# A hybrid DeltaNet, band attention and MoE block: the order of the v and vb projections, of the modulation matvecs, of the z tiles, and the pieces of the last expert loads

## The chip, the cores and the metric

The kernel runs on one core of one Trainium2 chip. The time is the device time of one execution, in microseconds. The kernel before takes 1188.68 us, the median of three runs (1187.45 to 1189.12).

## What is computed

The reference is one transformer block on 256 tokens of width 1024, all in f32. A conditioning vector gives six modulation rows (shift, scale and gate for each of two halves). The first half mixes the tokens, the second is a mixture of experts:

```python
mod = silu(c) @ w_ada + b_ada                      # sh1, sc1, ga1, sh2, sc2, ga2
h = rms_norm(x, norm_w[0]) * (1 + sc1) + sh1
proj = h @ w_in                                    # A: q, k, v, z, alpha, beta;  B: q, k, v
o_a = gated_delta_rule(l2(q), l2(k), v, g, beta)   # silu(conv(q, k, v)); chunks of 64, 4 heads of 128
o_a = rms_norm(o_a, a_norm_w) * silu(z)
o_b = chunk_band_attention(q_b, k_b, v_b, rel_bias)  # 8 heads of 64
x = x + ga1 * rms_norm(concat(o_a, o_b) @ w_out, norm_w[1])
h = rms_norm(x, norm_w[2]) * (1 + sc2) + sh2
gates, experts = top4(h @ w_router + b_router)     # 32 experts
y = sum_e gate_e * (swiglu(h @ w_up[e] + b_up[e]) @ w_down[e] + b_down[e])
x = x + ga2 * rms_norm(y, norm_w[3])
```

## The kernel before, in words

**Buffers.** Ten fixed blocks of 2 MiB (w0, w1, wA to wH), each with an f32 and an f32r view of the same bytes, take every weight. In the first part they hold projection weights and scratch; later they are a ring for expert weights in the order wB, wA, w0, wE, wF, wD, wC, w1, wG, wH (`RINGTAGS`). PSUM has three pools of banks: "mm" (3), "dl" (3) and "tp" (2).

**The stream of projections** (`stream`, L413). Weights come in halves of 256 columns. `split` (L210) writes each half as a high part (ScalarE) and a low part (VectorE and GpSimd). One projection tile is `mm3` (L231): 24 matmuls of 256 columns. Sixteen tiles follow k and q: qb, kb, vb, v, four each, at positions 1 to 16; z has four more. v's tiles pass through a convolution into `vT`; vb's are only copied; vb's weights lie in wD, v's in w0, z's in w1. For every third half the high part lies in `whx`, the second half of wH (f32r); others lie in wG and the first half of wH, z's first half among these.

**The modulation chunks** (`lates`, L517). Eight 2 MiB chunks of `w_ada` are loaded and reduced by `modrow` (L484): 16 matmuls at L203, a copy, 4 small products at L208. Seven share wF, so a load waits for the matvec before it. `ADAPOS` names the tile position at which chunk i is loaded and its matvec is written, right behind each other.

**The delta rule** (`chain`, L533) is written after position 16, with high priority. After the decays it inverts a triangular matrix by six doublings in `pair_mm` (L638, matmuls L642, two "dl" banks each). After doublings 3 and 4, `ktv` (L649) transposes k (L653) and v (L657), the latter into a "dl" bank. Then come L706 and L709, the products L731 to L757, and the outputs `oa`.

**Attention** (`attention`, L760) first loads a strip of relative biases into the second half of wH (L762); GpSimd masks it (L764). Then nine steps: three `scores` (L776, two "mm" banks each; VectorE adds the strip at L781 and so frees the banks), three `trans` (L800), three `av` (L815). `mixed` (L859) lays z tiles between the steps: `ZPOS` [0, 2, 0, 0] puts three before the first step and one before the third. w_out's B half is loaded into wD (L857) and split into wF and wD; when z is done, its A half is loaded into w1 (L872) and split (`spa`, second part in the first half of wH). `wout_b` (L830) is four tiles of 12 matmuls. From L1051 on, `wout_a`, residual, router and the first gather stand in an order written out by hand for TensorE and VectorE.

**The experts.** 14 groups of two, one or four experts; a group has six steps j of weights (four up, two down), one 2 MiB block per expert and step. The first group's experts are fixed, so its loads need no routing, only free blocks. `LAST` cuts the loads of the last group into pieces, interleaved between its two experts.

Outside L1051 to L1094 each engine's order comes from a scheduler that plays the program through a timeline before the run: what was written earlier goes first among what is ready, and high priority goes before all. SyncE issues every DMA in one queue.

The change touches L30 to L35, L207 to L238, L387, L415 to L436, L513 to L518, L649 to L659 and L696.

Of the kernel before, what the change touches and what calls it, by code (L numbers as in the profile page):

```python
# [26 lines left out]
KV = 2  # L27
ADA = list("PPPPPPPP")
ADATAG = list("FFBFFFFF")
ADAPOS = [0, 2, -1, 4, 6, 8, 10, 12]  # L30
ADABANK = "tp"
KW = 2
ZPOS = [0, 2, 0, 0]

LAST = {3: (4, 4), 4: (4, 4), 5: (2, 2, 2, 1, 1)}  # L35


SINGLES, QUADS = 2, 3
# [11 lines left out]
def block_kernel(ctx, tc, x, small, rows, rel_ext, wpre, wexp, b_up, b_down, out,  # L50
# [35 lines left out]
    def wload(i, tag):  # L86
        t = block(tag)
        nc.sync.dma_start(t, wpre[i])
        return t.rearrange("p (k n) -> p k n", k=8)
# [108 lines left out]
    def colvec(w, vec, out_cols, tag="dl"):  # L198
# [8 lines left out]
        for m in range(4):  # L207
            T.matmul(out_cols[:, m:m + 1], ev[:, m * 128:(m + 1) * 128], ind, start=True, stop=True)  # L208

    def split(w, kv=None, steps=1, extra=None, copy=None):  # L210


        sr, wl = w
        kv = kv or KV
        wh = extra
        if wh is None:
            wh = highs[nsp[0] % 3]
            nsp[0] += 1
        kn = sr.shape[1]
        wh = wh.rearrange("p (k n) -> p k n", k=kn)  # L220
        st = kn // steps
        for k in range(0, kn, st):
            (copy or S.copy)(wh[:, k:k + st], sr[:, k:k + st])
            m = k + kv // steps
            V.tensor_sub(wl[:, k:m], sr[:, k:m], wh[:, k:m])
            w_ = max(1, 512 // sr.shape[2])
            for i in range(m, k + st, w_):
                G.tensor_sub(wl[:, i:i + w_], sr[:, i:i + w_], wh[:, i:i + w_])
        return wh, wl

    def mm3(b_, lhs, rhs, ks=8, late="l", first=True, last=True):  # L231


        low = (1, 0) if late == "l" else (0, 1)
        seq = [(i, j, k) for k in range(ks) for i, j in ((0, 0), (1 - low[0], 1 - low[1]))]
        seq += [(*low, k) for k in range(ks)]
        for n, (i, j, k) in enumerate(seq):
            T.matmul(b_, lhs(i, k), rhs(j, k), start=first and n == 0, stop=last and n == len(seq) - 1)  # L238

    blC = block("wC")  # L240
    qbT, kbT = [blC[:, 1024 * i:1024 * i + 1024].rearrange("p (h t) -> p h t", h=4) for i in range(2)]
# [105 lines left out]
    whx = h2(1)  # L347
# [36 lines left out]
        G.tensor_mul(zg[:, a, sl].rearrange("p (h d) -> p h d", h=2), zg[:, a, sl].rearrange("p (h d) -> p h d", h=2),  # L384
                     rw[:, None, R_AN:R_AN + 128].to_broadcast([P, 2, 128]))

    halves = [(nm, hf) for nm in ("k", "q", "qb", "kb", "vb", "v", "z") for hf in range(2)]  # L387

    def evac(nm, h, b_):
        if nm == "qb":  # L390
# [22 lines left out]
    def stream():  # L413

        def sp(n):  # L415
            if n < len(halves):
                nm, hf = halves[n]
                sps[n] = split(ws[nm][hf], extra=whx if n % 3 == 2 else None)

        def after(at):  # L420
            if at == ("qb", 3):
                ws["v"] = hload(9, "w0")
            if at == ("kb", 3):
                ws["z"] = hload(10, "w1")
            if at in (("q", 3), ("v", 3), ("z", 3)):
                flush()
# [5 lines left out]
        for part in range(2):  # L432
            if part:
                with tc.high_priority():
                    hpath(1)
                ws["vb"] = hload(8, "wD")  # L436
                sp(2)
            for h in range(4):
                wx, m = sps[h // 2], h % 2
# [70 lines left out]
            T.transpose(rb[:, m * 128:(m + 1) * 128], mcs[seg][:, 4 * hf + m:4 * hf + m + 1].to_broadcast([P, P]), ident)  # L510
        S.copy(dst[:, hf * 512:hf * 512 + 512], rb)

    def late(jobs):  # L513
        for i, tag in jobs:
            modrow(i // 2, i % 2, wload(11 + i, tag))

    def lates(pos):  # L517
        late([(i, "w" + ADATAG[i]) for i in range(8) if ADAPOS[i] == pos])  # L518

    bias_parts()  # L520
    st_ = stream()
# [11 lines left out]
    def chain():  # L533
# [113 lines left out]
        kdt, wT = mem.tile([P, 2, 512], F32, tag="ga2", name="kdt").rearrange("p i (h d) -> i p h d", h=4)  # L647

        def ktv(a):  # L649
            sl = slice(4 * a, 4 * a + 4)  # L650
            kp = bank("dl")
            for h in range(4):
                T.transpose(kp[:, h * 128:(h + 1) * 128], kqT[:, h, 0, a * 128:(a + 1) * 128], ident)  # L653
            V.tensor_mul((kdt, kw)[a], kp.rearrange("p (h d) -> p h d", h=4), (kd, ew)[a][:, :, None].to_broadcast([P, 4, 128]))
            vp = bank("dl")
            for h in range(4):
                T.transpose(vp[:, h * 128:(h + 1) * 128], vT[:, h, a * 128:(a + 1) * 128], ident)  # L657
# [12 lines left out]
        for s_ in range(1, 6):  # L670
# [23 lines left out]
                ktv(s_ - 3)  # L694
            yield 0.6
        qd = kqT[:, :, 1, 128:256]  # L696


        def both(dst, src, scale, r_):
# [710 lines left out]
```

## Time and profile before

| | us |
|---|---|
| median of three runs | 1188.68 |
| profiled execution, its own time | 1189.61 |
| its span, first to last instruction | 1187.8 |
| TensorE matmul busy | 1036.5 (87%) |
| VectorE, ScalarE, GpSimd busy | 315.4, 194.2, 94.4 |
| DMA: share of 16 engines | 90.8% |
| mean granted TensorE clock | 0.948 |

The terms of the prediction come from the profiled execution, which has 1.8 us around its span and lies 0.9 us above the median. Its first 260 us are projections, delta rule, attention and router; then come the experts, whose 192 blocks of 2 MiB are most of the 451.91 MB moved.

### The profile page before, as it was taken

The page shows a single profiled execution, that of the slowest core. Times are in us where ns is not written, and L with a number is a line of the kernel's source. Part 1 is how long each engine was busy: PE and PEld are TensorE (multiplying, and loading weights), DVE is VectorE, ACT ScalarE, POOL GpSimd, SP SyncE. Part 2 cuts the span into 40 slices and gives each one's busy share as a digit, 9 for nine tenths or more (in the row PEclk, how much of TensorE's full clock was granted, in tenths as well). Part 3 has the DMA queues.
Part 4 walks back from the last instruction along what each step waited for, and adds up shares of the span by engine and source line. Part 5 has one row for each costly group of instructions (what it writes and reads, how often), then busy time and mean ns, then how long its engine had stood idle before and what let it go on. Part 6 is the DMA issues. An engine that isn't in the chain of part 4 may idle for free.

```text
span 1187.8 us, 14569 instructions
## 1 busy us (share of the span) xinstructions
PE 1036.5 (87%) x5945; PEld 499.0 (42%) x5945; DVE 315.4 (27%) x802; ACT 194.2 (16%) x387; POOL 94.4 (8%) x89
## 2 busy tenths in 40 slices
PE   4899999899966799999977798999966799989986
PEld 2688888654321234434431142435421243324231
DVE  5476356454103022121211012122111011111112
ACT  3554335331000001010100001011000001010101
POOL 1546334100000000000000000000000000000000
PEclk9899999989987899999997899999987899999998
DMA  9936545769999999999999999999999999999993
GB/s 363 402 100 267 214 167 214 306 274 399 410 429 428 428 411 429 427 429 427 428 426 429 428 427 428 426 430 427 429 426 428 427 429 427 428 427 429 428 419 150
DMA packets 37348, 451.91 MB, mean 380 GB/s; under 512 B 4192, under 2 KB 5856, under 8 KB 8096
## 3 DMA queue, kind: packets, MB, share of 16 engines
q1 hardware_dynamic: 37280, 450.96, 90.8%
q8 instruction: 48, 0.79, 0.3%
q14 instruction: 20, 0.16, 0.0%
HBM read 449.50 MB, written 1.05 MB: 379 GB/s over the span
## 4 chain that ended last, share of the span: by engine, by line
PE 56%; DMA 38%; DVE 2%; ACT 2%; issue 1%; SPq 0%; POOL 0%; DVEq 0%; ACTq 0%
PE dl L1122 23%; DMA wA_f<-in_wexp_dram 11%; DMA wH_f<-in_wexp_dram 9%; PE mm L1122 9%; DMA wE_f<-in_wexp_dram 7%; PE mm L238 7%; DMA wD_f<-in_wexp_dram 6%; DMA w_f<-in_wexp_dram 3%; PE mm L1174 2%; PE tp L1011 2%; PE dl L642 2%; PE tp L203 1%; PE mm L442 1%; PE dl L238 1%; PE dl L203 1%
## 5 line engine op out<-in xcount | busy, mean ns | idle before, releaser
L1122 PE MATMUL dl<-w_f,xg 128*64 128x512 f32 (+2 forms) x224 | 108.6, 636 | 4.1 <-DMA w_f<-in_wexp_dram 4.1
L1181 DVE TENSOR_TENSOR acc<-acc,mm 128x512 f32<-128x512 f32 x50 | 34.4, 689 | 253.8 <-PE mm L1174 253.8
L1122 PE MATMUL mm<-w_f,xg 128*64 128x512 f32 (+1 forms) x208 | 92.4, 594 | 0.0
L1286 POOL TENSOR_TENSOR wC_f<-acc,m_row 128x512 f32<-128x512 f32 x2 | 2.5, 1276 | 934.0 <-DMA wA_f<-in_wexp_dram 934.0
L1140 ACT ACTIVATE sg<-gm 128x512 f32<-128x512 f32 x28 | 17.6, 630 | 298.6 <-DVE gm L1138 281.1
L1122 PE MATMUL dl<-wF_f,xg 128*64 128x512 f32 (+1 forms) x128 | 61.1, 622 | 4.0 <-DMA wF_f<-in_wexp_dram 4.0
L1122 PE MATMUL dl<-wD_f,xg 128*64 128x512 f32 (+1 forms) x128 | 60.4, 622 | 4.0 <-DMA wD_f<-in_wexp_dram 4.0
L1174 PE MATMUL mm<-yg,wts 128*128 128x512 f32 x108 | 52.6, 614 | 12.6 <-ACT yg L1172 12.6
L1122 PE MATMUL dl<-wA_f,xg 128*32 128x512 f32 (+1 forms) x96 | 51.2, 693 | 10.2 <-DMA wA_f<-in_wexp_dram 10.2
L1122 PE MATMUL dl<-wE_f,xg 128*64 128x512 f32 (+2 forms) x112 | 56.9, 662 | 3.6 <-DMA wE_f<-in_wexp_dram 3.6
L1122 PE MATMUL mm<-wB_f,xg 128*64 128x512 f32 (+2 forms) x128 | 57.2, 595 | 0.0
L1122 PE MATMUL mm<-wA_f,xg 128*64 128x512 f32 (+2 forms) x128 | 57.1, 595 | 0.0
L1122 PE MATMUL dl<-wB_f,xg 128*32 128x512 f32 (+1 forms) x96 | 52.7, 702 | 4.3 <-DMA wB_f<-in_wexp_dram 4.3
L1172 ACT COPY yg<-dl 128x512 f32<-128x512 f32 x28 | 16.4, 585 | 241.1 <-PE dl L1122 241.1
L1122 PE MATMUL dl<-wC_f,xg 128*64 128x512 f32 (+2 forms) x112 | 51.8, 610 | 3.9 <-DMA wC_f<-in_wexp_dram 3.9
L1011 PEld LDWEIGHTS tp<-oh,x 128*128 128x128 f32 x432 | 50.6, 194 | 7.6 <-issue 6.9
L1011 PE MATMUL tp<-oh,x 128*128 128x128 f32 x432 | 53.4, 280 | 0.0
L1122 PE MATMUL mm<-wE_f,xg 128*64 128x512 f32 (+1 forms) x112 | 49.8, 595 | 0.3 <-DMA wE_f<-in_wexp_dram 0.3
L1122 PEld LDWEIGHTS dl<-w_f,xg 128*64 128x64 f32 (+2 forms) x224 | 31.2, 144 | 40.5 <-issue 33.2
L1021 DVE TENSOR_SCALAR xg<-tp,mc,mc 128x128 f32<-128x128 f32 x52 | 19.6, 406 | 94.1 <-PE dl L1122 87.8
L1138 DVE TENSOR_SCALAR gm<-dl 128x512 f32<-128x512 f32 x14 | 9.7, 692 | 130.0 <-PE dl L1133 121.7
L1019 ACT ACTIVATE xg<-tp,mc,mc 128x128 f32<-128x128 f32 x52 | 21.8, 454 | 132.2 <-DVE xg L1021 132.2
(625 smaller groups left out, 2256.6 us busy)
## 6 DMA issues: line engine op xcount, KB each, us to landing
w_f<-in_wexp_dram SPq DMA_DIRECT2D x37, 2048.0 KB, 33.6
wF_f<-in_wexp_dram SPq DMA_DIRECT2D x19, 2048.0 KB, 31.6
wD_f<-in_wexp_dram SPq DMA_DIRECT2D x19, 2048.0 KB, 35.0
wE_f<-in_wexp_dram SPq DMA_DIRECT2D x19, 2048.0 KB, 36.0
wA_f<-in_wexp_dram SPq DMA_DIRECT2D x18, 2048.0 KB, 37.9
wB_f<-in_wexp_dram SPq DMA_DIRECT2D x18, 2048.0 KB, 33.6
wG_f<-in_wexp_dram SPq DMA_DIRECT2D x18, 2048.0 KB, 30.8
wC_f<-in_wexp_dram SPq DMA_DIRECT2D x18, 2048.0 KB, 32.3
```

The costliest lines, as they stand in the source:

```text
L203: T.matmul(b_[32 * i:32 * i + 32, :], vec[:, k:k + 1].to_broadcast([P, 32]), w[:, k, :], start=k < 4, stop=k >= 4)
L238: T.matmul(b_, lhs(i, k), rhs(j, k), start=first and n == 0, stop=last and n == len(seq) - 1)
L442: T.matmul(bs[h], wx[i][:, k, m * 128:(m + 1) * 128], hx[j][:, k, :], start=k + n == 0, stop=k == 7 and n == 2)
L642: T.matmul(b_[r_, c_ * 64:c_ * 64 + 64], lhs[r_, c_, :], id64[r_, :] if rhs is None else rhs[r_, c_, r_] if rhs is U else rhs[r_, c_, :], ...
L1011: T.matmul(b_[:, k * 128:(k + 1) * 128], x2[:, a, half(n)][:, k * 128:(k + 1) * 128], oh[:, a], start=a == tiles[0], stop=a == tiles[-1])
L1019: S.activation(xg[:, k], src, AF.Identity, scale=mc, bias=sc)
L1021: V.tensor_scalar(xg[:, k], src, mc, sc, op0=ALU.mult, op1=ALU.add)
L1122: T.matmul(b_[i * n:(i + 1) * n, :], lhs[:, k, i * n:(i + 1) * n], w(k), start=k == 0, stop=last and k == 7)
L1140: S.activation(sg, gm, AF.Sigmoid, scale=1.702)
L1172: S.copy(yg, b_)
L1174: T.matmul(cb, wt[:, a], yg, start=not (last and nn), stop=True)
L1181: V.tensor_add(acc[:, a, sl], acc[:, a, sl], cb)
```

## The change

Six edits. (1) v is projected before vb: v's weights go to wD, vb's to w0, so v has positions 9 to 12. (2) v's transposes and their products leave `ktv` and stand behind the last doubling, as `vtv`. (3) `ADAPOS` moves chunks 3 to 7 later, and each late chunk's matvec is written two positions behind its load (`ADALAG`). (4) That matvec is bound behind the last projection matmul written so far, `issue_after` (an order on TensorE alone, no wait). (5) `ZPOS` becomes [2, 4, 6, 8]: one z tile before the third, fifth, seventh and ninth step of attention. The condition on "z" in `sp` alters nothing, since z's halves are numbers 12 and 13 and only n % 3 == 2 is concerned. (6) In the last group the loads of j = 2 come in two pieces each instead of one, those of j = 4 in four instead of two.

```diff
-ADAPOS = [0, 2, -1, 4, 6, 8, 10, 12]
+ADAPOS = [0, 2, -1, 5, 7, 10, 12, 14]
+ADALAG = 2
-ZPOS = [0, 2, 0, 0]
+ZPOS = [2, 4, 6, 8]
-LAST = {3: (4, 4), 4: (4, 4), 5: (2, 2, 2, 1, 1)}
+LAST = {2: (4, 4), 3: (4, 4), 4: (2, 2, 2, 2), 5: (2, 2, 2, 1, 1)}
...
+    lastmm = [None]
...
-            T.matmul(b_, lhs(i, k), rhs(j, k), start=first and n == 0, stop=last and n == len(seq) - 1)
+            lastmm[0] = T.matmul(b_, lhs(i, k), rhs(j, k), start=first and n == 0, stop=last and n == len(seq) - 1)
...
-    halves = [(nm, hf) for nm in ("k", "q", "qb", "kb", "vb", "v", "z") for hf in range(2)]
+    halves = [(nm, hf) for nm in ("k", "q", "qb", "kb", "v", "vb", "z") for hf in range(2)]
...
-                sps[n] = split(ws[nm][hf], extra=whx if n % 3 == 2 else None)
+                sps[n] = split(ws[nm][hf], extra=whx if n % 3 == 2 and nm != "z" else None)
...
-                ws["v"] = hload(9, "w0")
+                ws["vb"] = hload(8, "w0")
...
-                ws["vb"] = hload(8, "wD")
+                ws["v"] = hload(9, "wD")
...
-    def late(jobs):
-        for i, tag in jobs:
-            modrow(i // 2, i % 2, wload(11 + i, tag))
+    lw = {}
 
     def lates(pos):
-        late([(i, "w" + ADATAG[i]) for i in range(8) if ADAPOS[i] == pos])
+        for i in range(8):
+            if ADAPOS[i] == pos:
+                lw[i] = wload(11 + i, "w" + ADATAG[i])
+            if ADAPOS[i] + (ADALAG if ADAPOS[i] >= 0 else 0) == pos:
+                if lastmm[0] is None:
+                    modrow(i // 2, i % 2, lw[i])
+                else:
+                    with tc.issue_after(lastmm[0].ins if hasattr(lastmm[0], "ins") else lastmm[0]):
+                        modrow(i // 2, i % 2, lw[i])
...
         def ktv(a):
-            sl = slice(4 * a, 4 * a + 4)
...
+        def vtv(a):
+            sl = slice(4 * a, 4 * a + 4)
             vp = bank("dl")
...
         qd = kqT[:, :, 1, 128:256]
+        for a in range(2):
+            vtv(a)
```

## Rows read from the trace of the kernel before

**Rows 1.** Stretches: PE, PEld, DVE, ACT, POOL busy (x instructions), PE clock, DMA share, GB/s.

```profile
57.00:221.00 164.00, 163.58 (x1637) 140.17 (x1638) 95.63 (x211) 74.06 (x151) 70.86 (x58) 1.00 0.51 192
...
260.00:265.00 5.00, 5.00 (x20) 1.58 (x18) 0.00 (x0) 0.34 (x1) 0.00 (x0) 1.00 0.00 0
...
600.00:800.00 200.00, 167.98 (x832) 63.28 (x825) 34.30 (x78) 16.12 (x32) 0.00 (x0) 0.93 1.01 428
```

**Rows 2.** SyncE's queue, timeline: the first load into a block that an expert freed.

```profile
265.66 0.33 SPq L1113 DMA_DIRECT2D wB_f<-in_wexp_dram  x1
```

**Rows 3.** TensorE, timeline: k's transposes of the third doubling, and the fourth doubling.

```profile
132.53 0.66 PE L653 MATMUL dl<-ident,kqT 128*128 128x128 f32 x4
...
158.14 1.15 PE L642 MATMUL dl<-wE_f,lmrow 64*64 64x64 f32 x32
```

**Rows 4.** The bias strip: SyncE's wait (ns, then start in us); GpSimd's mask, timeline.

```profile
L762 SPq EVENT_SEMAPHORE  x1: 22945/22945/22945, 151.4 to 151.4; - x1
...
180.51 1.49 POOL L764 TENSOR_SCALAR wH_f<-wH_f 64x512 f32<-64x512 f32 x1 [1.31 <-DMA wH_f<-in_rel_ext_dram]
```

**Rows 5.** TensorE, timeline: last reads of whx (first row), of z's part in wH (second).

```profile
161.63 0.72 PE L238 MATMUL mm<-wA_r,wH_r 128*128 128x256 f32 x4
...
173.07 1.20 PE L238 MATMUL mm<-wH_r,wA_r 128*128 128x256 f32 x8
```

**Rows 6.** A matvec and scores on TensorE (timeline); GpSimd's share of wD's splits (group).

```profile
163.47 1.92 PE L203 MATMUL tp<-wF_f,csil 128*32 128x512 f32 x16
...
182.70 1.57 PE L776 MATMUL mm<-wC_f 64*128 64x128 f32 x12
...
L228 POOL TENSOR_TENSOR wD_r<-wD_f,wF_r 128x512 fp32r<-128x512 f32 x4 | 5.2, 1301 | 19.4 <-DVE wD_r L225 16.0 <-PE mm L238 3.3
```

**Rows 7.** TensorE in the first tiles of wout_a (timeline), and one stretch with its clock.

```profile
227.82 3.69 PE L238 MATMUL dl<-wH_r,wC_r 128*128 128x512 f32 x8 [2.63 <-POOL wH_f L919]
...
232.26 1.98 PE L238 MATMUL mm<-wG_r,wC_r 128*128 128x512 f32 x8
...
228.00:230.00 2.00, 2.00 (x5) 1.63 (x6) 0.00 (x0) 0.00 (x0) 0.00 (x0) 0.50 0.99 426
```

**Rows 8.** Timeline: load of w_out's A half, a run of wout_b, the last split.

```profile
192.12 1.09 SPq L94 DMA_DIRECT2D w_f<-in_wpre_dram  x2
...
202.70 2.14 PE L238 MATMUL mm<-wF_r,wC_r 128*128 128x512 f32 x8
...
209.21 1.27 POOL L228 TENSOR_TENSOR w_r<-w_f,wH_r 128x512 fp32r<-128x512 f32 x1
```

**Rows 9.** TensorE in the last group, timeline, to its last expert matmul.

```profile
1137.21 0.38 PE L1133 MATMUL mm<-bup,sel 96*64 96x512 bf16 x1
...
1140.08 0.64 PE L1122 MATMUL dl<-wD_f,xg 128*64 128x512 f32 x1 [0.26 <-DMA wD_f<-in_wexp_dram]
...
1154.09 0.38 PE L1133 MATMUL dl<-bup,sel 96*64 96x512 bf16 x1
1155.98 0.66 PE L1150 MATMUL tp<-ident,gm 128*128 128x128 f32 x4 [1.50 <-DVE gm L1144]
...
1174.05 0.59 PE L1122 MATMUL dl<-wA_f,aT__5966 128*64 128x512 f32 x1
```

**Rows 10.** When j = 3 is whole (TensorE's weight load waits for its last piece).

```profile
1150.23 0.14 PEld L1122 LDWEIGHTS dl<-w_f,xg 128*64 128x64 f32 x1 [0.29 <-DMA w_f<-in_wexp_dram]
```

**Rows 11.** A load of 512 KiB and its time to landing; the last load, likewise; GB/s.

```profile
L1113 SPq DMA_DIRECT2D wA_f<-in_wexp_dram x1: 333/333/333, 1155.0 to 1155.0; - x1
...
DMA to landing us min/median/max: 12.4/12.4/12.4
...
L1113 SPq DMA_DIRECT2D wA_f<-in_wexp_dram x1: 337/337/337, 1162.6 to 1162.6; - x1
...
DMA to landing us min/median/max: 7.4/7.4/7.4
...
1160.00:1165.00 5.00, 5.00 (x20) 1.50 (x19) 0.00 (x0) 0.00 (x0) 0.00 (x0) 1.00 0.95 365
```

## The prediction

> **What bounds the kernel now.** I read the table of stretches first. From 600 to 800 us the DMA engines are full at 428 GB/s; TensorE is not. From 57 to 221 us it is the other way round: TensorE is busy 163.58 of 164 us, DMA half of the time [rows 1]. Next the two are tied together. The ten blocks of the ring fill before any expert runs; from 260 to 265 us nothing moves [rows 1], and SyncE issues the next load at 265.66, when the first expert's matmuls have freed a block [rows 2]. From there the stream is nearly unbroken to the end, so the date of that first free block sets the end, and TensorE sets that date. A microsecond that TensorE loses or gains before 265 us is one of the whole; loads that come a few microseconds earlier or later are not. Last I read the timeline of the final group: TensorE ends its expert matmuls at 1174.6 us [rows 9], while the last load, issued at 1162.6, lands 7.4 us later, at 1170.0 [rows 11]. There TensorE lags the DMA by 4.6 us, and 3.7 of these can be won at most, since the last piece still needs four matmuls, 0.9 us at the pace of j = 2 and 3, two times 32 matmuls from 1140.08 to 1154.5 [rows 9].
>
> So two places count: TensorE's queue before 221 us, and the last 40 us.
>
> **The change, part by part.**
>
> v before vb, v's transposes behind the doublings. Today the doublings stop: k's transposes of the third stand at 132.5 us, the fourth begins at 158.1, when v exists [rows 3]. The change removes that stop. It is worth nothing by itself: TensorE did other tiles meanwhile, it is full, and no instruction goes away. The loads of v and vb swap blocks with equal bytes and equal positions. What it does is move the delta rule's work ahead of tile 16, and so tile 16 and all that hangs on it some 10 us later. Sum: 0; if the cover went, the two transposes and products would cost a few tenths.
>
> The matvecs, two positions later and bound. The count is the same, 1.92 us for each run of 16 matmuls [rows 6]. 2 MiB take 4.9 us at 428 GB/s [rows 1]; two tiles are 48 matmuls, at 8 in 1.2 us [rows 5] some 6 to 7 us, with chain work between. Bounds: nothing (no wait of TensorE on wF stands in the trace now) and 2 us in all, if landings come late; I take 0. A load in SyncE's queue still waits for the matvec before it, and behind it stand the w_out load and the strip, which are not ready earlier. But the last chunk's matvec now follows tile 16, and wF is the block that takes w_out's high part; so the splits of w_out's B half, with four GpSimd pieces of 1.3 us [rows 6], move from the stretch before the strip into the stretch in which the strip arrives.
>
> The z tiles, later. This is where I expect the loss. The strip's load waited 22.9 us, to 174.4 [rows 4]. Its own half of wH, whx, was last read at 162.4; what ended at 174.3 were z's matmuls on the other half [rows 5]. The same pattern stands at 227.8: TensorE waits 2.63 us for GpSimd's write of the second half of wH before it reads the first [rows 7]. So the two views of wH are ordered as one object. Today three z tiles come first and run while the strip loads. After the change the strip comes first, two z tiles must wait for it and its mask, and the scores, ahead of z in priority, take all three "mm" banks, which only VectorE's addition of the strip gives back. From the strip's issue at 174.35 to the end of its mask are 7.6 us [rows 4]; about 1.0 of it lies before tile 16 ends (the last 8 matmuls no longer read whx), so 6.6 us remain. In them TensorE has the matvec, 1.9, and 20 of the 32 score matmuls, 2.6 at 12 in 1.57 us [rows 6]: a gap of 2.1 us. Bounds: 0, if the rest of the delta rule is still there to fill it, and 7.3, if all four GpSimd pieces (5.2 us) run ahead of the mask. I take 2.1, since some of the delta rule will fill it and some pieces will stretch it. After the 2.63 us of idling at 227.8 the clock stood at 0.50, its 1.2 GHz level, and eight matmuls took 3.69 us for 1.98 [rows 7]: 1.7 us more. After a gap of this size I take 0.6, between 0 and 1.7. Sum: +2.7.
>
> The rest of attention has z and wout_b for cover, some 23 us of TensorE work, against engines that work through three jobs of scores; I take 0. Loads for the experts that become late here have about 9 us, the idle stretch to 265.66, to hide in.
>
> The last group. j = 2 in halves lets TensorE start at 1137.6 rather than 1140.08 [rows 9], but j = 3 is whole only at 1150.2 [rows 10], and half of it has then still to run; today it ends at 1154.5 [rows 9]. So j = 2 brings 0.4. j = 4 in quarters brings more: TensorE waits 1.50 us at 1155.98 for the second half of the activation [rows 9], and with quarters the first two of eight steps of j = 4, 1.7 us of matmuls, have landed by then and fit there. Together 1.9; bounds 0.4 (the queue's order keeps the wait) and 3.7 (above). The six more issues cost SyncE 0.33 us each [rows 2]; it runs 7 us and more ahead, so they are hidden.
>
> Small pieces could slow the stream. From 1150.2 to 1167.4 [rows 10, 11] seven MiB land, j = 4 and six pieces of 512 KiB: 427 GB/s, the full rate; only with the 256 KiB pieces does a stretch show 365 [rows 11]. The Trainium skill (DMA: Bandwidth & Descriptors, Rules for kernel authors) asks for at least 1 MiB per DMA for full bandwidth, which speaks against this edit. By that rule the sum would lose the 1.9 and by the row it keeps them; the trace does not bear the rule out.
>
> **Sum.** +2.7 - 1.9 = +0.8 us. The profiled execution (1189.61) lies 0.9 above the median, so 1190.4 there and 1188.7 + 0.8 = 1189.5 in the median.
>
> **The rivals.**
>
> (a) The gap is covered: the delta rule's last products, or a queue order that keeps z where it was (the change then does not do what it says), fill it. For it: the whole delta rule has high priority, and TensorE idled only 0.4 us in 164 [rows 1]. Then only the last group counts: 1186.8, and 1185.0 with its best bound.
>
> (b) The gap is wide and the kernel slower. One mechanism: GpSimd takes w_out's pieces ahead of the mask. Two pieces make the gap 4.7, with the half clock 1.7 after it: +4.5 net, 1193.2; all four 1195.8. It decides when the gap and what the clock costs pass 4.3 us. For it: the splits are written before attention and so go first. Against it: they wait for the matvec and for ScalarE.
>
> (c) w1 is late. From the load of w_out's A half, at the end of z, to its last split are 18.4 us today [rows 8]. With z at the end of attention the cover is the last av and wout_b, 48 matmuls at 8 in 2.0 us [rows 8], about 13 us. Up to 5 us of wait plus the clock, less the last group: about 1192.8. Against it: z's matmuls fill any idle moment and will not all stand last.
>
> (d) The small pieces run at 365 GB/s [rows 11]: j = 4 takes 11.5 us for 9.9, and the last group brings 0.3 for 1.9: 1191.1. The rule above says this; the landings say otherwise.
>
> **How the numbers follow.** Forecast 0.42, (a) 0.28, (b) 0.20, (c) 0.08, (d) 0.02. A measurement of this kernel can tell about 0.2%, 2.4 us, from no change. The forecast's own range is 1187.0 to 1192.0: 0.05 of it is faster, 0.28 the same, 0.09 slower. (a) gives 0.17 to faster and 0.11 to the same, where the last group brings less than 2.4. (b) and (c) give 0.26 to slower and 0.02 to the same, (d) 0.02 to the same. Faster 0.22, the same 0.43, slower 0.35. The range takes in (a) to near its best bound and (b) with two to three pieces: 1185.6 to 1194.5.
>
> **What would show it.** In the profile after: the fourth doubling right behind the third, and the delta rule's last matmuls before tile 16 ends or soon after (step one). No z matmul between the strip's issue and its mask, and TensorE idle there by about 2 us, the mask named as releaser or VectorE's addition behind it, with a lower clock after it. The first free block's load at about 268.4 instead of 265.66. In the last group no wait at the second transposes and the last expert matmul about 2 us nearer to the last landing. If TensorE has no gap before 221 us, (a) holds; if the load of the first free block is at 270 or later, (b) or (c), told apart by whether the time went at the strip or before wout_a. The prediction is wrong altogether if that load comes earlier than 265, since I see nothing that lets TensorE finish the first part sooner.

## The result, and the profile after

The changed kernel takes **1200.35 us** (median of 4 runs, 1200.09 to 1204.13) against 1188.42 us for the kernel before on the same chip (4 runs). The ratio is 1.0109, 95% interval 1.0093 to 1.0126: slower by about 1%, 11.9 us by the medians and 13.0 by the ratio. The forecast was 1189.5 us, in a range of 1185.6 to 1194.5.

The profiled execution took 1200.43 us, its span is 1198.3 us, 10.5 longer than before. The first question is where that lies. The date that set the end before, the first load into a block that an expert freed [rows 2], has moved from 265.66 to 277.50 us (SyncE's timeline of the changed kernel):

```profile
277.50 0.33 SPq L1126 DMA_DIRECT2D wB_f<-in_wexp_dram  x1
```

That is 11.84 us, more than the whole loss. The last expert matmul, at 1174.05 before [rows 9], comes 10.4 us later (TensorE, last group, changed kernel):

```profile
1161.73 0.64 PE L1135 MATMUL dl<-w_f,xg 128*64 128x512 f32 x1 [0.51 <-DMA w_f<-in_wexp_dram]
...
1184.02 1.02 PE L1135 MATMUL dl<-wA_f,aT__5966 128*64 128x512 f32 x2
```

It ends at 1185.04, before it ended at 1174.64. So the last group, or what lies between, gave back 1.4, and the 1.50 us wait for the second half of the activation [rows 9] is gone. The loss is all ahead of 277.50. One row per kernel over the stretch from 57 us to that load says what kind of time it is (columns as in [rows 1]); first the kernel before, then the changed one:

```profile
57.00:265.66 208.66, 201.27 (x1843) 166.53 (x1843) 118.15 (x301) 87.73 (x189) 73.42 (x60) 0.97 0.57 221
```

```profile
57.00:277.50 220.50, 208.23 (x1832) 167.91 (x1829) 115.54 (x299) 86.00 (x189) 71.92 (x59) 0.96 0.54 210
```

TensorE runs the same program in both (1843 and 1832 records; a few are missing from a trace), but is busy for 7.0 us more and idle for 12.27 us in place of 7.39, which is 4.9 more. Nothing was added to its work, so the longer busy time has to be the same matmuls spread over more time. Two groups of instructions give most of it. The late matvecs, over this stretch (instructions | busy us, mean ns | idle before), before and after:

```profile
L203 PE MATMUL tp<-wF_f,csil 128*32 128x512 f32 x112 | 14.5, 599 | 0.0
```

```profile
L204 PE MATMUL tp<-wF_f,csil 128*32 128x512 f32 x112 | 19.7, 600 | 0.0
```

The mean of one matmul is the same, 600 ns, the group is 5.2 us longer: fewer of them ran side by side. The timeline of the changed kernel shows why:

```profile
154.60 1.04 PE L204 MATMUL tp<-wF_f,csil 128*32 128x512 f32 x2
155.57 1.14 PE L651 MATMUL dl<-wB_f 64*64 64x64 f32 x16
156.65 0.55 PE L668 MATMUL dl<-ident,wB_f 128*128 128x128 f32 x3
157.12 1.05 PE L204 MATMUL tp<-wF_f,csil 128*32 128x512 f32 x4
158.11 0.55 PE L668 MATMUL dl<-ident,wB_f 128*128 128x128 f32 x3
158.58 1.90 PE L204 MATMUL tp<-wF_f,csil 128*32 128x512 f32 x10
```

A whole matvec is 16 records in 1.92 us [rows 6]. Here one is cut into 2, 4 and 10, because the delta rule's matmuls, of high priority, stand between; two records alone take 1.04 us. The second group are the doublings (L642 before, L651 after): 15.2 and 7.4 us before, 16.1 and 7.7 after in their two large forms, 1.2 us more, in the same manner: 32 records together take 1.15 us at [rows 3], and 16 alone 1.14 (155.57, above). That leaves 0.6 us of the 7.0. The lower mean clock (0.96 for 0.97) accounts for about as much: its low level costs 2.4 us at the strip (below), where it cost 1.7 at 227.82 [rows 7].

The idle time stands in two places. The first is the strip (timeline of all engines):

```profile
183.59 1.05 PE L769 MATMUL dl<-lmrow,wE_f 128*128 128x128 f32 x8
...
185.91 1.12 PE L241 MATMUL mm<-w_r,wA_r 128*128 128x256 f32 x8
186.15 0.39 SPq L775 DMA_DIRECT2D wH_f<-in_rel_ext_dram  x1
...
192.96 1.49 POOL L777 TENSOR_SCALAR wH_f<-wH_f 64x512 f32<-64x512 f32 x1 [32.48 <-DMA wH_f<-in_rel_ext_dram]
194.47 1.89 DVE L794 TENSOR_TENSOR w_f<-mm,wH_f 128x512 f32<-128x512 f32 x3 [11.38 <-POOL wH_f L777]
195.22 1.81 PE L789 MATMUL mm<-wC_f 64*128 64x256 f32 x4 [3.21 <-DVE w_f L794]
...
196.96 3.78 PE L241 MATMUL mm<-wH_r,wA_r 128*128 128x256 f32 x16
200.54 1.91 PE L241 MATMUL mm<-w_r,wA_r 128*128 128x256 f32 x8
...
204.29 2.18 PE L241 MATMUL mm<-wH_r,wA_r 128*128 128x256 f32 x16 [0.18 <-DVE w_f L794]
```

The delta rule's last products (L769) run at 183.6, before tile 16 has ended (L241, 185.91). In the kernel before they are L756 and follow the attention's last matmuls (L815), and the copy behind them ended at 213.06:

```profile
210.25 1.09 PE L815 MATMUL mm<-w_f,wC_f 128*64 128x128 f32 x14
211.27 1.16 PE L756 MATMUL dl<-lmrow,wE_f 128*128 128x128 f32 x8
```

The strip's load is issued at 186.15, when tile 16 has read its block for the last time; before it was 174.35. From there the strip has to land, be masked and be added, and TensorE stops for 3.21 us. In the next five microseconds it has nearly its low level of clock, 1.2 GHz; the z tile at 196.96 and its last eight matmuls at 200.54 take 3.78 and 1.91 us there, the same work later 2.18 (204.29) and 1.12 (210.56), 2.4 us less:

```profile
190.00:195.00 5.00, 2.02 (x14) 1.54 (x14) 0.53 (x1) 2.38 (x2) 1.49 (x1) 1.00 0.17 57
195.00:200.00 5.00, 4.78 (x18) 4.00 (x19) 5.00 (x10) 1.75 (x9) 2.27 (x2) 0.55 0.01 2
```

The second place is ahead of the fourth tile of `wout_b`. w_out's A half is loaded when z's last tile has read w1, at 218.79 for 192.12 [rows 8]; its last split, GpSimd's, ends at 237.56, and ScalarE's copy of a finished tile of `wout_b` (L851) waits for it, since that split reads the first half of wH and the copy writes the second:

```profile
234.96 2.60 POOL L231 TENSOR_TENSOR w_r<-w_f,wH_r 128x512 fp32r<-128x512 f32 x2 [4.62 <-DVE w_r L228]
...
237.60 1.08 ACT L851 COPY wH_f<-mm 128x512 f32<-128x512 f32 x2 [1.96 <-POOL w_r L231]
...
238.24 2.12 PE L241 MATMUL mm<-wF_r,wC_r 128*128 128x512 f32 x8 [3.23 <-ACT wH_f L851]
```

This takes the place of the stop of 2.63 us at 227.82 [rows 7].

### The profile page after: what moved, and what is told of

It is laid out like the page before. It is cut to its first block, busy times and chain, and to the rows that moved or that the text cites. A ratio compares the mean times of both kernels' runs of the same rounds, so it can differ in the third digit from the quotient of the medians.

```text
span 1198.3 us, 14596 instructions
## 1 busy us (share of the span) xinstructions
PE 1042.6 (87%) x5945; PEld 492.0 (41%) x5945; DVE 313.6 (26%) x802; ACT 194.1 (16%) x387; POOL 94.6 (8%) x89
## 3 DMA queue, kind: packets, MB, share of 16 engines
HBM read 449.50 MB, written 1.05 MB: 376 GB/s over the span
## 4 chain that ended last, share of the span: by engine, by line
PE 65%; DMA 27%; DVE 4%; ACT 2%; issue 1%; POOL 0%; SPq 0%; ACTq 0%; DVEq 0%; POOLq 0%
PE dl L1135 27%; PE mm L1135 12%; DMA wH_f<-in_wexp_dram 9%; DMA wA_f<-in_wexp_dram 8%; PE mm L241 7%; DMA wE_f<-in_wexp_dram 4%; PE mm L1187 3%; PE tp L1024 3%; DMA wD_f<-in_wexp_dram 3%; PE dl L651 2%; DMA w_f<-in_wexp_dram 2%; PE tp L204 2%; PE tp L1163 1%; PE dl L204 1%; ACT yg L1185 1%
## 5 line engine op out<-in xcount | busy, mean ns | idle before, releaser
L1135 PE MATMUL dl<-wA_f,xg 128*32 128x512 f32 (+1 forms) x96 | 46.9, 644 | 10.5 <-DMA wA_f<-in_wexp_dram 10.5
L1135 PE MATMUL dl<-wB_f,xg 128*32 128x512 f32 (+1 forms) x96 | 48.5, 654 | 3.8 <-DMA wB_f<-in_wexp_dram 3.8
L1135 PE MATMUL mm<-wH_f,xg 128*64 128x512 f32 (+1 forms) x96 | 42.4, 594 | 0.3 <-DMA wH_f<-in_wexp_dram 0.3
```

The lines of the kernel that those rows point to most:

```text
L1135: T.matmul(b_[i * n:(i + 1) * n, :], lhs[:, k, i * n:(i + 1) * n], w(k), start=k == 0, stop=last and k == 7)
```

## The experiments

The theories on trial. **A**: the loss is made of several pieces. It splits in two: **A1**, the pieces themselves (cut matvecs, doublings in smaller runs), and **A2**, TensorE's order: since v no longer holds the delta rule back, its end goes ahead of the last projection tiles; these, the strip and the attention come later, and the delta rule's end, which had stood beside the attention, is used up (A2 took this form after the first round). **B**: w_out's A half, loaded late. **C**: the binding makes TensorE wait for a matvec's load. **D**: v's order costs by itself, whatever else is done.

All ratios are against runs of the kernel before on the same chip. The microseconds are the ratio minus one, times 1188.4; the last four columns are dates in the profiled execution, one for each kernel; that of e2 took 4.1 us more than its kernel's median, e12's 2.7 and e5's 2.5 more, e16's 2.4 less.

| kernel | ratio (95%) | us | strip issued | delta rule ends | attention's last matmul ends | first freed block |
|---|---|---|---|---|---|---|
| before | 1 | 0 | 174.4 | 213.1 | 211.3 | 265.7 |
| the change | 1.0109 (1.0093 to 1.0126) | +13.0 | 186.2 | 185.3 | 221.9 | 277.5 |
| e1 change, z tiles back | 1.0176 (1.0159 to 1.0193) | +20.9 | 195.3 | 185.7 | 230.2 | 284.1 |
| e2 change, matvecs whole | 1.0067 (1.0050 to 1.0084) | +8.0 | 184.3 | 184.4 | 217.8 | 275.9 |
| e3 change, matvecs back | 1.0091 (1.0074 to 1.0107) | +10.8 | 189.1 | 191.9 | 219.9 | 277.2 |
| e4 v's order alone | 1.0121 (1.0104 to 1.0138) | +14.4 | 195.0 | 191.2 | 228.8 | 278.7 |
| e5 v's order, strip freed | 1.0056 (1.0040 to 1.0073) | +6.7 | 147.2 | 189.5 | 222.6 | 271.6 |
| e6 change, strip freed | 1.0001 (0.9990 to 1.0013) | +0.1 | 145.5 | 187.3 | 215.6 | 265.5 |
| e7 before, strip freed | 0.9960 (0.9947 to 0.9972) | -4.8 | 139.7 | 212.1 | 210.3 | 259.1 |
| e8 last group alone | 0.9992 (0.9982 to 1.0001) | -1.0 | 174.6 | 213.5 | 211.7 | 266.0 |
| e9 change, v's order back | 1.0025 (1.0010 to 1.0040) | +3.0 | 160.1 | 206.3 | 209.0 | 267.5 |
| e10 z tiles alone | 1.0051 (1.0034 to 1.0068) | +6.1 | 161.7 | 212.9 | 213.0 | 269.6 |
| e11 matvecs alone | 0.9982 (0.9971 to 0.9992) | -2.1 | 171.9 | 205.6 | 209.1 | 259.7 |
| e12 change, whole and freed | 0.9938 (0.9916 to 0.9960) | -7.4 | 142.7 | 184.6 | 213.8 | 261.1 |
| e13 hold, misplaced | 1.0114 (1.0099 to 1.0130) | +13.5 | 189.0 | 188.1 | 224.1 | 279.9 |
| e14 before, freed, matvecs, last group | 0.9940 (0.9926 to 0.9953) | -7.1 | 139.4 | 208.4 | 211.7 | 259.3 |
| e15 as e14, matvecs whole | 0.9922 (0.9908 to 0.9935) | -9.3 | 137.1 | 207.6 | 211.6 | 257.4 |
| e16 change, v held | 1.0044 (1.0031 to 1.0058) | +5.2 | 170.5 | 196.9 | 211.3 | 268.2 |

**First round: which part is it?**

**e1**, z tiles back:

```diff
-ZPOS = [2, 4, 6, 8]
+ZPOS = [0, 2, 0, 0]
```

> The changed kernel with the four z tiles back at their old places (two ahead of the attention's third step, as before); all else as changed. Theory A (the loss is made of several pieces: late matvecs cut apart by the delta rule's matmuls, about +4.9 us; TensorE's idle 3.2 us and the half clock behind it, about +3.3 us, where the z tiles no longer stand in front of the strip; the doublings' own matmuls in smaller pieces, about +1.2): the stop at 190 to 195 us and the half clock at 195 to 205 us go, the matvecs stay cut, so 1193.5 to 1195.5 us. Theory B (all of the loss is w_out's second half, loaded only when the last z tile has read its block): the whole loss goes, about 1188.5 us, with the gain between 220 and 245 us. Theory C (the binding makes TensorE wait for the matvecs' loads): no change, about 1200 us.

Measured: 1208.14 us, eight more, the wrong side of all three theories. SyncE's wait for the strip (ns, then start) grows from 6953 to

```profile
L775 SPq EVENT_SEMAPHORE  x1: 15640/15640/15640, 179.6 to 179.6; - x1
```

because z's tiles, now ahead of the strip again, read the other half of wH, as before [rows 5]. They do not cover the strip; they delay it. With v first, the later z tiles are a gain.

**e2**, matvecs whole (`colvec`, only the late ones):

```diff
+            with tc.high_priority() if tag == "tp" else contextlib.nullcontext():
-            T.matmul(b_[32 * i:32 * i + 32, :], vec[:, k:k + 1].to_broadcast([P, 32]), w[:, k, :],
-                     start=k < 4, stop=k >= 4)
+                T.matmul(b_[32 * i:32 * i + 32, :], vec[:, k:k + 1].to_broadcast([P, 32]), w[:, k, :],
+                         start=k < 4, stop=k >= 4)
```

> The changed kernel with the eight matmuls of a late matvec given the same high priority as the delta rule's, so that nothing is put between them (all eight matvecs stand whole in TensorE's queue; their loads and the binding as changed). Theory A: about 0.95 us less for each of the six cuts, so 1195 to 1196.5 us, with a matvec's 16 records at 1.9 us each and the rest of the loss (the strip's stop) still there. Theory B (w_out's late load): no change, 1199.5 to 1201 us. Theory C (binding makes TensorE wait): no change or slower, 1200 us or more.

Measured: 1196.64 us, 5.0 less than the change by the ratios, as A had it. The group of matvecs, at 19.7 us in the change, now has

```profile
L206 PE MATMUL tp<-wF_f,csil 128*32 128x512 f32 x112 | 13.5, 598 | 0.0
```

So a cut matvec costs what the timeline says, but that is a part only; 8 us of loss remain.

**e3**, matvecs back:

```diff
-ADAPOS = [0, 2, -1, 5, 7, 10, 12, 14]
-ADALAG = 2
+ADAPOS = [0, 2, -1, 4, 6, 8, 10, 12]
+ADALAG = 0
...
-                if lastmm[0] is None:
+                if True:
```

> The changed kernel with the matvecs where they were (old places, no lag behind the load, no binding); v's order, the z tiles and the last group as changed. Two cuts are left in place of six. Theory A: 4 cuts fewer, 1196 to 1197.5 us, with the strip's stop still there. Theory C (lag and binding are what costs): about 1189 us. Theory B: no change, 1199.5 to 1201 us.

Measured: 1198.77 us, 2.1 less than the change by the ratios, with intervals that overlap. Theory C is out: without lag and binding nearly all of the loss stays. A's range, 1196 to 1197.5, is missed too: the matvecs take 15.5 us for 19.7, as it had them, but the doublings 16.9 and 8.5 us, 1.6 more.

**e4**, v's order alone: `halves`, the two `hload`s and `vtv` as in the change, put into the kernel before.

> The kernel before with v's tiles ahead of vb's and v's transposes behind the doublings, and nothing else of the change: matvecs, z tiles and the last group as before. Theory A: two more cuts of matvecs (+1.9) and smaller pieces of the doublings (+1.2) against an earlier start of the projections (-1.75): 1188.5 to 1191 us. Theory B and C: as before, 1188.4 us. If v's order itself is what costs (rival D: the delta rule without its stop takes TensorE from the projections, whatever the matvecs do): 1195 us or more.

Measured: 1202.70 us. This run carries the round: v's order by itself costs 14.4 us, more than the whole change, as theory D had it (1195 or more) and far above A's 1188.5 to 1191. The pieces are less than a third of it: its matvecs take 15.5 us, 1.0 more than before, its doublings 17.6 and 8.5, 3.5 more. What stands out is the stretch beside the attention, the same 30 us in the kernel before and in e4:

```profile
200.00:230.00 30.00, 26.95 (x169) 22.59 (x168) 13.59 (x44) 13.91 (x38) 7.32 (x6) 0.96 0.77 306
```

```profile
200.00:230.00 30.00, 21.21 (x125) 16.41 (x124) 20.64 (x55) 18.08 (x60) 13.79 (x13) 0.77 0.38 145
```

TensorE is idle for 8.8 us instead of 3.1, at a clock of 0.77, while VectorE and ScalarE work through the attention.

**Second round: the strip.** The strip is made free of what holds it. The halves of wH become objects of their own, and the last projection tile's high part goes to another buffer than the strip's half, so that the strip is loaded 35 us earlier in the kernel before (e7) and 41 to 48 earlier in the others (e6, e5):

```diff
+    hH = [[nc.alloc_sbuf_tensor_at(f"wH{i}_{d_}", (P, 2048), dt, offset=base + 16384 * 9 + 8192 * i).ap()
+           for d_, dt in (("f", F32), ("r", F32R))] for i in range(2)]
-    highs = [fixed["wG"][1][:, 0:2048], fixed["wG"][1][:, 2048:4096], fixed["wH"][1][:, 0:2048]]
+    highs = [fixed["wG"][1][:, 0:2048], fixed["wG"][1][:, 2048:4096], hH[0][1]]
...
-        return fixed["wH"][dt][:, 2048:4096]
+        return hH[1][dt]
...
-                sps[n] = split(ws[nm][hf], extra=whx if n % 3 == 2 else None)
+                sps[n] = split(ws[nm][hf], extra=whx if n % 3 == 2 and n < 11 else None)
```

**e5**, on v's order alone:

> v's order alone, as in the run that cost 14.5 us, but with the attention's strip freed: the two halves of block wH are objects of their own, so that the strip no longer waits for reads of the other half, and the last projection tile's high part no longer lies in the strip's half, so that the strip can be loaded from about 150 us on. Theory A2 (v's order lets the delta rule run ahead of the last projection tiles; the strip's load, which waits for those tiles, is issued at 195 in place of 174 us and nothing is left to stand in front of it): the stops and half clocks between 200 and 230 us go, about 8.8 - 3.0 us of idle PE and some 5 us of half clock, so 1189 to 1192 us. Theory A1 (cut matvecs and doublings in small pieces are the loss): 1199 us or more.

Measured: 1194.92 us, half of the loss. The strip is there at 152, but TensorE still stops, now for the attention's own steps:

```profile
205.00:210.00 5.00, 2.65 (x24) 1.88 (x24) 4.64 (x21) 5.00 (x19) 1.77 (x3) 1.00 1.04 441
210.00:215.00 5.00, 2.04 (x8) 1.43 (x8) 4.71 (x14) 3.67 (x6) 2.12 (x3) 0.66 0.61 262
215.00:220.00 5.00, 4.45 (x22) 3.62 (x23) 3.71 (x6) 1.90 (x1) 2.49 (x2) 0.50 0.00 0
```

ScalarE (5.00 of 5) and VectorE (4.64 and 4.71) are the busy ones. A2 had the direction; that a freed strip would bring all of it was wrong. The attention needs work beside it on TensorE, strip or no strip.

**e6**, on the changed kernel:

> The changed kernel with the same freeing of the strip. Theory A2: the 3.2 us stop at 192 us and the half clock behind it (3.3 us) go, the cut matvecs stay: 1193 to 1195 us. Theory B (w_out's second half is loaded late because its block waits for the last z tile): 1198 us or more, since that load stays where it is.

Measured: 1188.42 us (10 runs), no different from the kernel before. That is a larger gain than either theory gave. The 3.21 us stop and its half clock are gone, and so is the stop ahead of `wout_b`, though w_out's A half is still loaded late, at 214.70: with the halves of wH apart, the copy no longer waits for the split. Theory B is out in the form I gave it: not the late load held TensorE there but the order between two views of one block. In place of both stops a looser stretch is left (TensorE 4.41, 3.75 and 4.62 of 5 us from 195 to 210).

**e7**, on the kernel before:

> The kernel before with the same freeing of the strip, and nothing of the change. There the strip was no bound (it was issued at 174 us and TensorE did not stop for it), but the copy of the first attention output also waits for the other half of wH (2.63 us at 227.8, and 1.60 at 236.7): theory A2: 1184 to 1187.5 us. If these waits were only the last of several: 1188 us.

Measured: 1182.91 us (10 runs), 4.8 better than before. The stops of 2.63 and 1.60 us are gone. So about 5 us of the freeing are worth the same in both kernels, and some 8 us more are only there with the change. Which of its two edits brings how much was not tried.

**e8**, `LAST` alone:

```diff
-LAST = {3: (4, 4), 4: (4, 4), 5: (2, 2, 2, 1, 1)}
+LAST = {2: (4, 4), 3: (4, 4), 4: (2, 2, 2, 2), 5: (2, 2, 2, 1, 1)}
```

> The kernel before with the last expert group's loads in smaller pieces, and nothing else of the change. By the trace of the changed kernel, where the last expert matmul came 10.4 us later and the first free block 11.8 us later, the pieces give 1.3 us: 1186.8 to 1187.3 us. The prediction's term was 1.9 us: 1186.3. If small pieces slow the loads (rival d): 1189 us or more.

Measured: 1187.65 us (10 runs), by the ratio -1.0 with an interval from -2.1 to +0.1: a small gain, or none. The waits of 1.59 and 1.50 us for the activation are gone, but TensorE, further ahead, now runs into the loads:

```profile
1150.52 0.64 PE L1122 MATMUL dl<-w_f,xg 128*64 128x512 f32 x1 [1.33 <-DMA w_f<-in_wexp_dram]
```

**Third round: the parts alone, and the change without v.**

**e9**, the changed kernel with v's order undone (`halves`, `hload`s, `vtv(s_ - 3)` back in the doublings):

> The changed kernel with v's order undone (vb's tiles first, v's transposes at the fourth and fifth doubling); later and bound matvecs, later z tiles and the last group as changed. Theory A2 (with v's tiles last the delta rule has to stop for them, so the strip's block is free 12 us sooner and the delta rule's end runs beside the attention): the strip is issued at 163 to 175 us, the attention's last matmul ends by 212 us, and the time is 1186 to 1190 us. If the matvecs or the z tiles carry the loss by themselves (theories A1, C): 1196 us or more.

Measured: 1191.54 us (10 runs), +3.0. The attention's end is as A2 had it; the strip comes at 160.1, 3 us earlier than its range, and the time is 1.5 above its range. The remaining parts make that 3.0, as the next two show.

**e10**, `ZPOS` alone in the kernel before:

```diff
-ZPOS = [0, 2, 0, 0]
+ZPOS = [2, 4, 6, 8]
```

> The kernel before with the z tiles at their later places, and nothing else. The prediction's terms for this edit were +2.1 (the strip's gap) and +0.6 (half clock), bounds 0 to 9: 1190.6 us. Theory A2: in the kernel before the delta rule's end covers the strip, so no stop comes, and since no z tile reads block wH ahead of the strip, the strip is issued at about 164 in place of 174 us: 1184 to 1188 us.

Measured: 1195.20 us, +6.1, above the prediction's term and against A2's expectation. The strip is issued at 161.65, as foreseen, but TensorE then stops three times between 170.6 and 175.2 (0.41, 0.72 and 0.42 us), the clock stands at 0.50 from 175 to 180, and w_out's A half, loaded when the last z tile is done, is the next to be late:

```profile
210.67 0.80 SPq L94 DMA_DIRECT2D w_f<-in_wpre_dram  x2
...
230.31 2.12 PE L238 MATMUL mm<-wF_r,wC_r 128*128 128x512 f32 x8 [3.23 <-ACT wH_f L838]
```

An earlier strip had nothing to win: in the kernel before TensorE was busy for 133.00 of the 133 us from 57 to 190.

**e11**, `ADAPOS`, `ADALAG` and the binding alone in the kernel before:

> The kernel before with the matvecs later and bound, and nothing else. Its queue has two cuts in matvecs in place of one besides the first (2+6, 2+6 against 6+2): theory A: +1 us at the most, 1188 to 1189.5 us. Prediction's term: 0 (bounds 0 to 2). Theory C (the binding makes TensorE wait): 1192 us or more.

Measured: 1186.17 us (10 runs), -2.1 (-3.4 to -1.0): a small gain, where all theories and the prediction had none. `wout_a` no longer stops for the 2.63 us of [rows 7]:

```profile
223.57 2.14 PE L241 MATMUL dl<-wH_r,wC_r 128*128 128x512 f32 x8
```

Why the delta rule ends 7.5 us sooner in it was not followed further. The three parts without v's order add up: -2.1 + 6.1 - 1.0 = +3.0, what e9 measured; with intervals of 1 to 2 us on each, that it fits to the tenth is luck.

**e12**, the change with both mendings, those of e2 and e6:

> The changed kernel with both mendings: the matvecs whole (which gave 3.7 us by itself) and the strip freed (which gave 11.9). If the two losses are apart: 1184 to 1186 us, no better than the kernel before with the strip freed (1182.9). If the cut matvecs only filled time that the attention left idle anyway: 1187 to 1189 us.

Measured: 1181.87 us, -7.4. Against e6 that is 7.5 less: the cut matvecs cost no less on top of a freed strip, so the two losses are apart. The range for that, 1184 to 1186, lay too high. (The 3.7 and 11.9 in the expectation are differences of medians; by the ratios they are 5.0 and 12.8.)

**Fourth round: order or pieces?** The direct test of A2 keeps the change's order of tiles and all its waits, and only puts v's eight transposes, and so the delta rule's end, behind tile 16 on TensorE:

```diff
     steps(st_, 0, 16)
+    tile16 = lastmm[0]
...
+        with tc.issue_after(tile16.ins if hasattr(tile16, "ins") else tile16):
-        for a in range(2):
-            vtv(a)
+            for a in range(2):
+                vtv(a)
```

**e13** was this run with a slip: it took `lastmm[0]` inside `chain`, where the delta rule's own first matmul has already taken that place, long done. The order stayed as it was.

> The changed kernel with one edit: v's eight transposes (and so the delta rule's end) are queued on TensorE behind the last projection tile, as v's late tile held them back in the kernel before. The matvecs' eight cuts stay as they are. Order theory: the strip is issued at 170 to 178 us in place of 186, the delta rule's end lies beside the attention again, and the time falls by 6 to 9 us, to 1191 to 1194.5 us. Pieces theory: the strip may come sooner, but the time stays at 1198 us or more.

Measured: 1201.23 us, v's transposes at 159.5 to 167.8, the dates of the change some 3 us later. It decides nothing on the question; it gives the time of the change once more.

**e16**, with the right matmul:

> The changed kernel with v's eight transposes queued on TensorE behind the last matmul of the sixteenth projection tile (in the run before this one they were queued behind a matmul that had long been done, and nothing moved). The queue now has all of vb's matmuls ahead of v's transposes and the delta rule's end behind them, among the attention's; of the cuts in matvecs two fewer are left (2+6, 2+6, 7+1, 1+7). Order theory: the strip is issued at 168 to 176 us in place of 186, and the time falls by 6 to 9 us, two of them by the fewer cuts: 1191 to 1194.5 us. Pieces theory: only the fewer cuts count: 1198 to 1199 us.

Measured: 1194.49 us, ratio 1.0044 for 1.0109: 7.7 us less than the change. In the timeline tile 16 ends, the strip is issued, v's transposes follow, and the delta rule's last products run among the scores:

```profile
170.24 1.12 PE L241 MATMUL mm<-w_r,wA_r 128*128 128x256 f32 x8
170.47 0.39 SPq L776 DMA_DIRECT2D wH_f<-in_rel_ext_dram  x1
...
171.20 1.03 PE L668 MATMUL dl<-ident,wB_f 128*128 128x128 f32 x8
...
194.31 0.71 PE L770 MATMUL dl<-lmrow,wE_f 128*128 128x128 f32 x4
...
194.96 0.70 PE L790 MATMUL mm<-wC_f 64*128 64x256 f32 x2
...
195.58 0.71 PE L770 MATMUL dl<-lmrow,wE_f 128*128 128x128 f32 x4
```

Its row over the first part, to be read beside the two above:

```profile
57.00:268.15 211.15, 202.91 (x1833) 165.32 (x1831) 117.51 (x299) 85.39 (x189) 72.29 (x59) 0.98 0.57 219
```

TensorE is idle for 8.24 us in place of 12.27, and busy for 5.3 less. Of these, 2.1 are matvecs (17.6 for 19.7 us): the longer queue cuts fewer of them. The doublings keep their 16.1 and 7.7 us. Of the other 3.2, 3.1 are the projection matmuls on wH_r (8.8 for 10.6 us) and on w_r (9.5 for 10.8), at 287 ns each for 322 and 285 for 305: the z tiles that ran at the low clock behind the strip's stop in the change. From 168 to 220 us TensorE is idle for 0.15 us here, in the change for 3.66. So about 2 of the regained microseconds are pieces, and the larger part is order, as A2 had it. What of it comes from the earlier strip and what from the delta rule's end as cover, this run does not separate.

**A version that beats both.** **e14** joins the freed strip, the matvecs of the change and its last group on the old order of v and z; **e15** adds the whole matvecs of e2.

> The kernel before with the strip freed (-5.0 alone), the matvecs later and bound (-2.1 to -2.8 alone) and the last group's smaller pieces (-0.3 to -1.0 alone); v's order and the z tiles as before. If the gains add up: 1179 to 1181 us. If the matvecs' gain and the freed strip's are the same idle time: 1182 to 1183 us.

> As the run before it, with the late matvecs' eight matmuls at high priority, so that none is cut (here two are besides the first). If each cut costs about 0.95 us: 2 to 3 us less than that run, 1177 to 1179 us. If a whole matvec delays the delta rule by as much: no difference.

Measured: 1180.38 us (0.9940) and 1177.81 us (0.9922), 5 runs each. The first is 0.8 us short of the sum of its parts (-4.8 - 2.1 - 1.0 = -7.9 for -7.1), the second brings 2.1 more. e15 is 0.8% faster than the kernel before and 1.9% faster than the change. Its first part:

```profile
57.00:257.41 200.41, 195.43 (x1839) 163.31 (x1840) 115.14 (x303) 86.90 (x189) 74.30 (x60) 0.98 0.59 230
```

## Why the prediction was wrong

**What bounds the kernel** was right: the date of the first free block goes with the end from run to run, and TensorE's queue sets it. The table's last column goes with the ratios, within 4 us.

**The step that failed** is the first of the working, "v before vb": "It is worth nothing by itself: TensorE did other tiles meanwhile, it is full, and no instruction goes away ... Sum: 0". By e4 it is worth 14.4 us alone, and by the change against e9 10.0 beside the other parts. The same paragraph said that the edit moves "tile 16 and all that hangs on it some 10 us later", and it does: 11.8 us for the strip's issue. But it gave that no price, because TensorE was full [rows 1]. It still is in the change, up to 190 us, and stops behind that. The prediction did not ask what will be left beside the attention when the delta rule has gone ahead. The stop at [rows 3] had kept the delta rule's end for later, and beside the attention, from 179 to 211 us, that end was part of TensorE's other work. The attention itself hangs on ScalarE, VectorE and GpSimd; in the change and in e1 to e4 it ends 31 to 36 us after the strip is issued, wherever that lies. e16 shows it from the other side: the hold put back, 7.7 of the 13.0 us go. The cover is not all of it: with the strip freed the loss goes too, though the delta rule's end stays early (e6), while with v's order alone half of it stays (e5).

**The price of a matmul** is a second failure: work that changes places was taken to keep its time ("The count is the same, 1.92 us for each run of 16 matmuls"). The matvecs went from 14.5 to 19.7 us without one more instruction. Its bounds, "nothing" and "2 us in all, if landings come late", looked at their loads alone. Neither edit makes the six cuts by itself: the kernel before has one, v's order alone two (e4), the matvecs' places alone two (e11). Whole again, they bring 5.0 us (e2) or 7.5 (e12). The matvecs' edit itself is worth -2.1 on the kernel before (e11), below the lower bound.

**The z tiles**, "+2.7": the gap came where it was foreseen, 3.21 us for 2.1, named by VectorE's addition, and the clock after it went near its low level; for this the prediction had 0.6, with 1.7 as the bound, and the z matmuls at 196.96 to 202.4 show 2.4. But the term was worked out for the old order of v. There it is +6.1 (e10, inside its bounds of 0 to 9.0). In the change the sign turns: without the later z tiles the kernel is 8.0 us slower still (e1).

**The two views of wH ordered as one object**: right. Made two objects, and with the strip's half left free, before gains 4.8 us and the change 12.8.

**The last group**, "-1.9": the direction held, the size was nearer to 1.0 (e8), and no difference is within its interval. In the trace of e8 TensorE's lag behind the last landing falls from 4.6 to 3.0 us, and the last landing itself comes 0.8 later.

**The rivals.** (a) fell: TensorE was idle. (b) had the right side and the wrong mechanism: GpSimd masked the strip at 192.96 and took w_out's pieces for wD at 197.65 only. (c) was there in kind, 3.23 us before `wout_b` in place of 2.63 before `wout_a`, so it cost next to nothing net, and by e6 not through the load's date. (d) fell: e8 is not slower, and from the last landing of j = 3 to the last of j = 4 its eight pieces take 10.3 us, where four of 1 MiB took 9.9 before and (d) had 11.5. The Trainium skill (DMA: Bandwidth & Descriptors, Rules for kernel authors) asks for at least 1 MiB per DMA; the landings bear that out by these 0.4 us, where the prediction read no loss. Two of the prediction's sums are off: 48 matmuls at 8 in 1.2 us are 7.2 us, not 6 to 7, and the terms of (c) give 1192.4 or, with 1.7 for the clock, 1193.5, not 1192.8; nothing hangs on either. None of the rivals had v's order in it, and so the range ended 6 us below the measured time.

## What to carry to other kernels

A stall of a high-priority chain on a full engine may be what keeps its work for a later stretch that has none; before removing it, list what the engine will have beside the next latency-bound stage. Price each edit in the order that the other edits make, not in the old one: the same z tiles cost 6 us there and saved 8 here. And where two buffers share a block under two views, give each its own object before moving anything around them; together with keeping the last projection tile out of the strip's half, that was worth more (4.8 us) than any edit of this change.

## What the runs showed of the hardware

Where a run of small matmuls is cut decides its time. A matvec is eight matmuls of two records each, dealt in turn to four groups of 32 output columns. Its pieces take, by the number of records in them (timelines of before, the change, e4 and e5):

| records in the piece | 2 | 4 | 6 | 8 | 10 | 12 | 14 | 16 |
|---|---|---|---|---|---|---|---|---|
| us | 1.04 | 1.05 | 1.06 | 1.06 | 1.90 | 1.91 | 1.92 | 1.92 |

Up to four matmuls, one on each group, take no longer than one, and the next four take 0.86 more. A cut within a round of four makes the round be paid twice. The seven late matvecs on wF, always 112 records of 598 to 601 ns, were busy for:

| cuts in the seven matvecs | 0 (e2, e12, e15) | 1 (before) | 2 (e4, e11) | 3 (e9) | 4 (e16) | 6 (the change, e6) |
|---|---|---|---|---|---|---|
| us | 13.5 | 14.5 | 15.5 | 16.6 | 17.6 | 19.7 |

That is 1.03 us for each cut. A cut between the two rounds is nearly free: e5 has two cuts and 14.7 us, since its second falls behind the eighth record and costs 0.20:

```profile
150.53 1.06 PE L206 MATMUL tp<-wF_f,csil 128*32 128x512 f32 x8
151.53 2.18 PE L653 MATMUL dl<-wB_f 64*64 64x64 f32 x48
153.64 1.06 PE L206 MATMUL tp<-wF_f,csil 128*32 128x512 f32 x8
```

The Trainium skill (TensorE: Matmul & The Clock Gate, Part 3: Packing small matmuls — row/col tiling) says that small matmuls at different positions of the array run at the same time. The traces agree (eight records in 1.06 us, two in 1.04), and add that other matmuls queued between them end that overlap.
